# A residual-add LayerNorm on one core: the wait for the last store moves from SyncE's queue to TensorE's

## The chip, the cores and the metric

The kernel runs on one core of one Trainium2 chip. The metric is device time in microseconds (us), the median over several executions. With it comes, for every execution, the *span*: the time from the first to the last instruction of the kernel that the trace records. The device time is a little longer than the span, that difference called the *remainder* below. Spans of timed runs are given to 0.1 us, so the remainder of one run is good to 0.05 us, and a mean over several runs to less.

## The reference

```python
batch, seq, dim = 16, 1024, 512          # x and residual, float32
z = x + residual
mean = np.mean(z, axis=-1, keepdims=True)
var = np.var(z, axis=-1, keepdims=True)
return gamma * (z - mean) / np.sqrt(var + eps) + beta
```

The inputs are 2 x 33.55 MB and the output is 33.55 MB.

## The kernel before

SyncE issues all large transfers, GpSimd adds the residual, ScalarE takes the sums for mean and variance, VectorE normalises in place. TensorE does almost nothing: at the start it spreads gamma and beta over 128 partitions with two small matmuls. The kernel ends with SyncE waiting until the stores have landed and clearing all the semaphores that it used, so that the next execution finds zeros.

```python
OUT_CHUNKS = [16] * 7 + [8, 4, 4]            # rows per partition of each store
...
so = [sem(f"so{c}") for c in range(len(stores))]   # one semaphore per store, the last allocated
nums = [s.num for s in sems]
...
# TensorE: all that it does
nc.tensor.wait_ge(s_const, 1)
for k, dest in enumerate((gamma_p, beta_p)):
    nc.tensor.wait_ge(s_gb[k], 16)
    nc.tensor.matmul(dest[:, :], ones[:, :], gb_row[:, k * D : (k + 1) * D], start=True, stop=True
    ).then_inc(s_pe, 1)
...
# SyncE, after its last store was issued
for o, (lo, n) in enumerate(stores[:-1]):
    if lo >= stored:
        nc.sync.wait_ge(so[o], 16)
nc.sync.sem_clear(range(nums[0], nums[-1]))             # all but the last semaphore
nc.sync.wait_ge(so[-1], 16)                             # the last store
nc.sync.sem_clear(range(nums[-1], nums[-1] + 1))        # its semaphore
```

A store's semaphore reaches 16 by sixteen increments. In the trace those of the last store come one by one, from 236.15 to 238.33 us.

## Time and profile before

| | before |
|---|---|
| device time, median of the first 3 runs | 239.53 us (239.42 to 239.70) |
| the profiled run: time, span, remainder | 239.69, 238.37, 1.32 us |
| DMA queue q1, share of 16 engines | 99.1% |
| busiest compute engine (ScalarE) | 186.5 us, 78% |
| busy TensorE | 3.7 us |

The first lines are from the profile's page of the kernel before. The first gives the span, the second each engine's busy time and share; the DMA row shows the busy share of the DMA engines in 40 equal slices, in tenths; the last line is the queue's share.

```profile
span 238.4 us, 1803 instructions
PE 3.7 (2%) x4; PEld 1.2 (0%) x4; DVE 177.2 (74%) x290; ACT 186.5 (78%) x545; POOL 142.2 (60%) x21
...
DMA  8999999999999999999999999999999999999996
...
q1 hardware_dynamic: 6336, 100.67, 99.1%
```

The DMA engines are full in every slice but the first and the last, so the transfers bound the kernel, and the change doesn't touch them. The next view is the list of SyncE's own waits in the window from 228 us to the end: the waiting line, what it waited for, us in total, number of waits, the longest.

```profile
SPq L138 <- DVE zbuf L243: 5.9, 1, 5.9
SPq L166 <- DMA out_dram<-zbuf: 4.6, 2, 2.4
SPq L169 <- DMA out_dram<-zbuf: 2.3, 1, 2.3
```

L138 issues the last store once VectorE (DVE) is done; L166 are the waits for the stores before it, L169 the wait for the last. The instructions themselves, from the views of the two clearing lines: duration in ns (smallest, median, largest), and when the first and last of them started.

```profile
L167 SPq EVENT_SEMAPHORE_RANGE_CLEAR  x1: 118/118/118, 235.9 to 235.9; - x1
...
L169 SPq EVENT_SEMAPHORE_RANGE_CLEAR  x1: 25/25/25, 238.3 to 238.3; - x1
```

The wait itself is not part of the duration. The Trainium skill says so of such instructions ("Perfetto Trace Analysis", "Sequencer-only Instruction (DRAIN, etc)": the reported window is the execution alone, after the semaphores are satisfied), and this trace agrees: SyncE waited 2.3 us there and 25 ns are reported. The clear of L169 is the last instruction of the span.

One more view of the kernel before, the barrier at its opening (L55), lets one compare the engines at the same kind of instruction.

```profile
L55 SPq EVENT_SEMAPHORE  x2: 17/17/17, 1.5 to 1.8; - x2
...
L55 PEldq EVENT_SEMAPHORE  x2: 51/51/51, 1.5 to 1.8; - x2
```

PEldq is TensorE's sequencer. Its semaphore instruction takes three times as long as SyncE's.

### The profile page before, as it was taken

How to read it: one execution, taken by the hardware profiler on the slowest of the kernel's cores; microseconds unless marked ns; L12 is line 12 of the kernel's file. 1: busy time of each engine (PE TensorE's matmuls, PEld its weight loads, DVE VectorE, ACT ScalarE, POOL GpSimd, SP SyncE). 2: the span in 40 equal slices, each digit the busy share in tenths (PEclk: the TensorE clock that was granted, in tenths of full speed). 3: DMA queues.
4: the chain of work that ended last, by engine and by line, in shares of the span. 5: the costliest groups of instructions: out<-in, count | busy, mean ns of one | idle time of the engine just before them, and what ended most of it. 6: DMA issues, size and time to landing. Idle time of an engine off the chain costs nothing.

```text
span 238.4 us, 1803 instructions
## 1 busy us (share of the span) xinstructions
PE 3.7 (2%) x4; PEld 1.2 (0%) x4; DVE 177.2 (74%) x290; ACT 186.5 (78%) x545; POOL 142.2 (60%) x21
## 2 busy tenths in 40 slices
PE   0600000000000000000000000000000000000000
PEld 0100000000000000000000000000000000000000
DVE  0000488888888889998888888887888648888870
ACT  2003999999999999999999999989997399999700
POOL 0098988989889407893088930889209892770000
DMA  8999999999999999999999999999999999999996
GB/s 308 438 429 415 437 437 429 426 423 437 429 429 418 440 434 426 459 434 396 429 429 429 434 429 429 426 470 434 390 434 418 434 440 408 472 434 434 390 425 257
DMA packets 6340, 100.67 MB, mean 422 GB/s; under 512 B 706, under 2 KB 706, under 8 KB 708
## 3 DMA queue, kind: packets, MB, share of 16 engines
q1 hardware_dynamic: 6336, 100.67, 99.1%
q10 hardware_dynamic: 4, 0.00, 0.0%
HBM read 67.11 MB, written 33.55 MB: 422 GB/s over the span
## 4 chain that ended last, share of the span: by engine, by line
ACT 38%; DMA 33%; issue 10%; POOL 7%; ACTq 5%; DVE 3%; SPq 1%; DVEq 0%; POOLq 0%
DMA rbuf<-in_residual_dram 21%; ACT junk_s L203 20%; ACT junk_m L194 18%; DMA out_dram<-zbuf 12%; POOL zbuf L181 7%; ACTq L194 2%; DVE zbuf L228 2%; DVE zbuf L243 1%; ACTq L203 1%; SPq L138 1%; ACTq L189 1%; ACT std L211 0%; ACTq L201 0%; ACTq L210 0%; DVEq L228 0%
## 5 line engine op out<-in xcount | busy, mean ns | idle before, releaser
L181 POOL TENSOR_TENSOR zbuf<-zbuf,rbuf 128x4096 f32<-128x4096 f32 (+1 forms) x17 | 142.0, 8353 | 70.9 <-DMA rbuf<-in_residual_dram 70.9
L228 DVE SCALAR_TENSOR_TENSOR zbuf<-zbuf,nm,gamma_p 128x512 f32 x128 | 87.1, 743 | 50.4 <-ACT junk_s L203 50.4
L194 ACT ACTIVATE junk_m<-zbuf 128x512 f32 x128 | 74.9, 585 | 28.5 <-POOL zbuf L181 23.3
L203 ACT ACTIVATE junk_s<-zbuf,nm 128x512 f32 x128 | 88.8, 694 | 3.9
L243 DVE SCALAR_TENSOR_TENSOR zbuf<-zbuf,rstd,beta_p 128x512 f32 x128 | 87.1, 744 | 1.1
L203 ACT ACTIVATION_READ_ACCUMULATOR junk_s<-zbuf,nm x128 | 23.9, 187 | 0.0
L194 ACT ACTIVATION_READ_ACCUMULATOR junk_m<-zbuf x128 | 23.9, 187 | 0.0
L211 ACT ACTIVATE std<-ssq,eps_t x32 | 9.5, 297 | 3.7
L237 DVE RECIPROCAL rstd<-std x32 | 5.4, 170 | 0.0
L187 ACT ACT_TABLE_LOAD x1 | 1.3, 1283 | 2.7 <-PEq L55 2.7
L123 PE MATMUL gamma_p<-gb_row,ones 1*128 1x512 f32 x2 | 2.0, 1122 | 7.3 <-DMA gb_row<-in_gamma_dram 7.3
L123 PE MATMUL beta_p<-gb_row,ones 1*128 1x512 f32 x2 | 1.9, 1056 | 0.0
L118 DVE MEMSET ones<- 1x128 f32 x1 | 0.2, 165 | 2.0 <-PEq L55 2.0
L123 PEld LDWEIGHTS beta_p<-gb_row,ones 1*128 1x128 f32 x2 | 0.7, 332 | 1.0 <-DMA gb_row<-in_beta_dram 0.5
L123 PEld LDWEIGHTS gamma_p<-gb_row,ones 1*128 1x128 f32 x2 | 0.5, 305 | 7.3 <-issue 7.3
L278 POOL MEMSET const-float32-0.0<- 128x1 f32 x1 | 0.1, 99 | 0.2 <-issue 0.2
L278 POOL MEMSET const-bfloat16-1.0<- 128x1 bf16 x1 | 0.1, 101 | 0.0
L278 POOL MEMSET const-uint8-127<- 128x1 uint8 x1 | 0.1, 101 | 0.0
L278 POOL MEMSET const-float32-1.0<- 128x1 f32 x1 | 0.1, 98 | 0.0
L119 DVE MEMSET eps_t<- 128x1 f32 x1 | 0.1, 59 | 0.0
## 6 DMA issues: line engine op xcount, KB each, us to landing
zbuf<-in_x_dram SPq DMA_DIRECT2D x15, 2048.0 KB, 32.8
rbuf<-in_residual_dram SPq DMA_DIRECT2D x15, 2048.0 KB, 30.1
out_dram<-zbuf SPq DMA_DIRECT2D x7, 4096.0 KB, 28.6
zbuf<-in_x_dram SPq DMA_DIRECT2D x2, 1024.0 KB, 32.6
rbuf<-in_residual_dram SPq DMA_DIRECT2D x2, 1024.0 KB, 34.6
out_dram<-zbuf SPq DMA_DIRECT2D x1, 2048.0 KB, 15.0
out_dram<-zbuf SPq DMA_DIRECT2D x2, 1024.0 KB, 9.4
gb_row<-in_gamma_dram ACTq DMA_DIRECT2D x1, 2.0 KB
```

Source lines behind the costliest of these rows:

```text
L123: nc.tensor.matmul(dest[:, :], ones[:, :], gb_row[:, k * D : (k + 1) * D], start=True, stop=True).then_inc(s_pe, 1)
L138: i = nc.sync.dma_start(out=out, in_=in_).then_inc(s, 16)
L181: nc.gpsimd.tensor_tensor(out=z, in0=z, in1=part(rbuf, R_ROWS, a, an), op=ALU.add).then_inc(s_add, an)
L187: act.preload_act_table_set("sqrt_and_others")
L189: with act.Fori(0, turns) as t:
L194: act.activation(out=junk_m[k][:, :], in_=zbuf[:, bass.ds(zoff + k * D, D)], func=ACT.Identity, scale=-inv_d, accum_out=nm[:, bass.ds(r0 + ...
L203: act.activation(out=junk_s[k][:, :], in_=zbuf[:, bass.ds(zoff + k * D, D)], func=ACT.Square, bias=nm[:, bass.ds(r0 + k, 1)], accum_out=ss ...
L211: act.activation(out=std[:, bass.ds(r0, TURN)], in_=ssq[:, bass.ds(r0, TURN)], func=ACT.Sqrt, bias=eps_t[:, 0:1], scale=inv_d,).then_inc(s ...
L228: dve.scalar_tensor_tensor(out=row, in0=row, scalar=nm[:, bass.ds(r0 + k, 1)], in1=gamma_p[:, :], op0=ALU.add, op1=ALU.mult,)
L237: dve.reciprocal(out=rstd[:, bass.ds(r0, TURN)], in_=std[:, bass.ds(r0, TURN)]).then_inc(s_dve, TURN)
L243: dve.scalar_tensor_tensor(out=row, in0=row, scalar=rstd[:, bass.ds(r0 + k, 1)], in1=beta_p[:, :], op0=ALU.mult, op1=ALU.add,).then_inc(s_ ...
L278: nc = _bacc.Bacc("TRN2", target_bir_lowering=False, num_devices=1)
```

## The change

The last store's wait and the clear of its semaphore are issued on TensorE, which has had nothing to do since about 11 us. Nothing says that TensorE is better for it; the question is what the place of these two instructions is worth.

```diff
     nc.sync.sem_clear(range(nums[0], nums[-1]))
-    nc.sync.wait_ge(so[-1], 16)
-    nc.sync.sem_clear(range(nums[-1], nums[-1] + 1))
+    nc.tensor.wait_ge(so[-1], 16)
+    nc.tensor.sem_clear(range(nums[-1], nums[-1] + 1))
```

## The prediction

> **What bounds the kernel now.** The DMA engines. The page's row of DMA slices reads 9 tenths in 38 of 40 slices, queue q1 is busy 99.1% of 16 engines' span; no compute engine is over 78% (ACT 186.5 us, DVE 177.2, POOL 142.2, PE 3.7 of 238.4 us). The change touches no transfer, no arithmetic and no wait that frees a buffer.
>
> **The end as it stands** (instructions and semaphore events of the trace). The last normalise ends on DVE at 230.8 us, and the last 1 MB store is issued on SyncE at 230.81. SyncE then waits for the earlier stores (events at 233.38 and 235.82), clears all semaphores but the last at 235.91 (118 ns), and waits 2.3 us for the last store (list of SyncE's waits, L169). Fifteen of its sixteen increments are there by 236.81, the sixteenth at 238.33: one DMA engine lags with single 8 KB packets of 0.31 us until 237.87. The one-semaphore clear starts at 238.348, 15 ns after that increment, takes 25 ns, and is the span's last instruction.
>
> **What changes.** That clear leaves SyncE's stream and becomes TensorE's last instruction. TensorE, idle after the second gamma/beta matmul (about 11 us), parks on the last store's semaphore for some 227 us and delays nobody. SyncE is done 2.3 us earlier, after the big clear at about 236.0. The last store's landing is not moved.
>
> So only the reaction to the last increment and the clear itself change engine, some 40 ns in all, fully on the critical path. The opening barrier shows both at the same thing: released together (SyncE starts at 1.182 us, TensorE at 1.194), its semaphore instruction takes 17 ns on SyncE and 51 ns on TensorE. I estimate from this that reaction plus clear goes from 40 ns to 80 to 130 ns: +0.04 to +0.1 us in the span.
>
> **Outside the span.** The measured 239.53 us is 1.1 us longer than the span. The Trainium skill ("Runtime: NRT & Kernel Launch", "The ~15µs preamble/postamble breakdown") says that a barrier after the kernel waits for all engines. If so, only the last engine counts, and SyncE's being early gains nothing; this trace stops at the last clear and cannot show it. The ending may be longer or shorter on TensorE; with 1.1 us at stake, I give that at most half a microsecond either way.
>
> **Prediction.** 239.6 us, 8 in 10 within 239.2 to 240.0. Faster by over 2%: 0.01; within 2%: 0.98; slower by over 2%: 0.01. Two per cent is 4.8 us, twice the wait that moves.
>
> **What would show it right or wrong.** Right: the compute groups the same within 0.5 us; the last store issued at about 230.8 us and landed at about 238.3; SyncE's last instruction the big clear near 236.0; TensorE's clear within 0.15 us of the sixteenth increment and last in the span. The step "only reaction and clear change" is wrong if the last increment itself moves by over 0.3 us, or TensorE's clear starts late or takes over 0.2 us. The step on the time outside the span is wrong if measured time minus span leaves 1.1 us by over 0.3.
>
> **What would make it wrong.** A TensorE that wakes slowly after 227 us; an ending outside the trace that is dearer or cheaper on TensorE; the big clear on SyncE now ending its stream and letting something of the ending overlap the last 2.3 us (a gain of up to 1 us). None reaches 2%.

## The result and the profile after

| | before | after |
|---|---|---|
| device time, median of 4 runs | 239.49 us (239.42 to 239.70) | 239.97 us (239.77 to 240.39) |
| ratio after/before, 95% interval | | 1.0021 (1.0004 to 1.0038) |
| the profiled run: time, span, remainder | 239.69, 238.37, 1.32 us | 239.98, 238.39, 1.59 us |
| remainder, mean over the runs with both (least to most) | 1.32 (one run) | 1.58 (1.57 to 1.59, 4 runs) |

A ratio is the mean time of one kernel's fast runs over that of the other's fast runs of the same rounds, so it is not quite the ratio of the medians in the table. All runs were at a granted clock of 1.0. The experiments ran in three sets of rounds, on chips 7, 13 and 9; the remainder of the kernel before was 1.31, 1.31 and 1.30 us there, so remainders are compared across the sets.

The interval leaves 1 out: the changed kernel is slower by a fifth of a per cent. The page of the changed kernel, in the lines that answer to those above:

```profile
span 238.4 us, 1803 instructions
PE 3.7 (2%) x4; PEld 1.2 (0%) x4; DVE 177.2 (74%) x290; ACT 186.5 (78%) x545; POOL 142.2 (60%) x21
...
DMA  8999999999999999999999999999999999999996
...
q1 hardware_dynamic: 6336, 100.67, 99.1%
```

These are the same, digit for digit. SyncE's waits in the last 10 us have lost one row:

```profile
SPq L138 <- DVE zbuf L243: 5.9, 1, 5.9
SPq L166 <- DMA out_dram<-zbuf: 4.7, 2, 2.4
```

And from the views of the two clearing lines of the changed kernel:

```profile
L167 SPq EVENT_SEMAPHORE_RANGE_CLEAR  x1: 118/118/118, 235.9 to 235.9; - x1
...
L169 PEldq EVENT_SEMAPHORE_RANGE_CLEAR  x1: 63/63/63, 238.3 to 238.3; - x1
```

The clear stands on TensorE now and takes 63 ns in place of 25. And the instructions of the trace hold no more than that: the events of the two traces (instruction starts, and the increments of the last store's semaphore, in us) line up to 0.05 us, but for the fifteenth increment, which came 0.11 us earlier.

```
                                         before     after
last store issued by SyncE              230.811   230.770
fifteenth increment of its semaphore    236.806   236.696
sixteenth increment                     238.331   238.296
the clear starts                        238.348   238.324
the clear ends = end of the span        238.373   238.387
```

From the sixteenth increment to the end of the span it is 42 ns before and 91 ns after, 0.05 us more. The medians differ by 0.48 us. The rest is not in the instructions of the trace; between the two profiled runs 0.27 us of it is in the remainder. (The traces do hold semaphore events after the end of the span; they are read after the five points of the section on the prediction.)

### The profile page after: what moved, and what is told of

It is laid out like the page before. It is cut to its first block, busy times and chain, and to the rows that moved or that the text cites. A ratio compares the mean times of both kernels' runs of the same rounds, so it can differ in the third digit from the quotient of the medians.

```text
span 238.4 us, 1803 instructions
## 1 busy us (share of the span) xinstructions
PE 3.7 (2%) x4; PEld 1.2 (0%) x4; DVE 177.2 (74%) x290; ACT 186.5 (78%) x545; POOL 142.2 (60%) x21
## 4 chain that ended last, share of the span: by engine, by line
ACT 38%; DMA 33%; issue 10%; POOL 7%; ACTq 5%; DVE 3%; SPq 1%; DVEq 0%; POOLq 0%
DMA rbuf<-in_residual_dram 21%; ACT junk_s L203 20%; ACT junk_m L194 18%; DMA out_dram<-zbuf 12%; POOL zbuf L181 7%; ACTq L194 2%; DVE zbuf L228 2%; DVE zbuf L243 1%; ACTq L203 1%; SPq L138 1%; ACTq L189 1%; ACT std L211 0%; ACTq L201 0%; ACTq L210 0%; DVEq L228 0%
```

## The experiments

The theories:

- **A**: after its last instruction each engine has an ending that the trace doesn't show. TensorE's is longer than SyncE's.
- **B**: what costs is that SyncE is not the last any more, whoever takes its place.
- **C**: TensorE is slow because it was parked for 227 us.
- **N**: the difference is scatter of the DMA part.

Later A was divided: **P**, the endings run side by side and the last to finish counts; **S**, only the engine that comes last counts; **W**, the engine that the last store's semaphore releases counts; **Q**, a fixed addition whenever another engine than SyncE is released by the last store.

### The changed kernel again

No edit. It ran in the same rounds as the next three kernels and 11 runs of the kernel before.

> The changed kernel once more, unedited. Measured time minus span was 1.32 us for the profiled run of the kernel before and 1.58 us for that of the changed one. Theory A (after the last clear there is an ending that the trace doesn't show, and it is dearer when TensorE is the engine that comes last): time minus span 1.5 to 1.7 us in every run, time 0.2 to 0.5 us over the kernel before. Theory N (the 0.48 us between the medians was scatter of the DMA part): time minus span 1.3 us in some runs, time within 0.15 us of the kernel before.

Measured: 240.22 us median against 239.82 us, ratio 1.0014 (1.0001 to 1.0027). The mean span is 238.62 us against 238.58 us, so hardly different. The remainder is 1.60 us (1.57 to 1.63 in 5 runs) against 1.31 us (1.27 to 1.37 in 11 runs). The two ranges don't touch, although the times overlap. N falls as the cause of the remainder. The scatter of the time is in the span: the kernel before ranges over 0.9 us there, and a quantity that leaves the span out is much sharper.

### The last wait and clear on each other engine

The edit, here for ScalarE, placed after that engine's loop; VectorE (`nc.vector`) and GpSimd (`nc.gpsimd`) likewise.

```diff
     nc.sync.sem_clear(range(nums[0], nums[-1]))
-    nc.sync.wait_ge(so[-1], 16)
-    nc.sync.sem_clear(range(nums[-1], nums[-1] + 1))
 ...
+    nc.scalar.wait_ge(so[-1], 16)
+    nc.scalar.sem_clear(range(nums[-1], nums[-1] + 1))
```

> The last wait and clear on ScalarE, after its loop (it ends at about 225 us). Theory A1 (the ending depends on which engine comes last): a value of time minus span of its own, between 1.2 and 1.7 us, the same in every run. Theory B (what costs is that SyncE is no longer last and its early end helps nothing or harms): 1.58 us like TensorE. Theory C (TensorE is slow because it was parked for 227 us, cold): ScalarE worked until 225 us, so 1.3 us as SyncE. The clear itself starts within 0.1 us of the sixteenth increment under all.

> The last wait and clear on VectorE, after its loop (it ends at 230.8 us). Theory A1: a value of time minus span of its own, between 1.2 and 1.7 us. Theory B: 1.58 us. Theory C: 1.3 us. The clear takes 25 to 60 ns.

> The last wait and clear on GpSimd, after its last addition (it ends at about 213 us). Theory A1: a value of time minus span of its own, between 1.2 and 1.7 us. Theory B: 1.58 us. Theory C: 1.3 us, or a little over, since it is parked for 25 us.

The clears, one line from each kernel's view of its clearing line (ACTq is ScalarE, DVEq VectorE, POOLq GpSimd). ScalarE:

```profile
L252 ACTq EVENT_SEMAPHORE_RANGE_CLEAR  x1: 41/41/41, 238.3 to 238.3; - x1
```

VectorE:

```profile
L252 DVEq EVENT_SEMAPHORE_RANGE_CLEAR  x1: 55/55/55, 238.4 to 238.4; - x1
```

GpSimd:

```profile
L252 POOLq EVENT_SEMAPHORE_RANGE_CLEAR  x1: 48/48/48, 238.5 to 238.5; - x1
```

| last engine | sixteenth increment to end of span | remainder, mean (least to most) | runs | median time | ratio (95%) |
|---|---|---|---|---|---|
| SyncE (before) | 0.04 us | 1.31 (1.27 to 1.37) | 11 | 239.82 | |
| VectorE | 0.08 | 1.43 (1.40 to 1.48) | 5 | 239.92 | 1.0002 (0.9989 to 1.0015) |
| ScalarE | 0.06 | 1.48 (1.47 to 1.51) | 6 | 240.17 | 1.0023 (1.0004 to 1.0043) |
| TensorE | 0.09 | 1.60 (1.57 to 1.63) | 5 | 240.22 | 1.0014 (1.0001 to 1.0027) |
| GpSimd | 0.07 | 1.86 (1.81 to 1.90) | 6 | 240.36 | 1.0021 (1.0009 to 1.0034) |

The second column is from the profiled run of each kernel (the one of before is the first of the study). Each engine has a remainder of its own, steady to 0.06 us about its mean. That is what A expects, although GpSimd's 1.86 us lies outside the 1.2 to 1.7 us that were forecast for it. B wants one value for the four that are not SyncE, and they range from 1.43 to 1.86 us. C wants SyncE's value for the engines that worked almost to the end; VectorE, busy until 230.8 us, has 1.43 us and GpSimd has the largest of all. The medians and ratios do not order the engines: ScalarE's ratio is the largest because three of its six runs happened to have spans of 238.9 to 239.7 us. Nor is the order that of the visible clear: GpSimd's clear is shorter than VectorE's and TensorE's, and its remainder is the longest.

### TensorE woken before the end

VectorE signals a new semaphore after its loop, and TensorE does one more matmul on that signal, before it waits for the last store. In this and in all the kernels below the new semaphore `s_late` is allocated after the stores' semaphores, and the last clear covers both.

```diff
-    nc.sync.sem_clear(range(nums[0], nums[-1]))
-    nc.sync.wait_ge(so[-1], 16)
-    nc.sync.sem_clear(range(nums[-1], nums[-1] + 1))
+    nc.sync.sem_clear(range(nums[0], nums[-2]))
+    nc.tensor.wait_ge(s_late, 1)
+    nc.tensor.matmul(gamma_p[:, :], ones[:, :], gb_row[:, 0:D], start=True, stop=True)
+    nc.tensor.wait_ge(so[-1], 16)
+    nc.tensor.sem_clear(range(nums[-2], nums[-1] + 1))
 ...
+    late_t = nc.alloc_sbuf_tensor("late_t", [P, 1], FP32)      # after VectorE's loop
+    nc.vector.memset(late_t[:, :], 0.0).then_inc(s_late, 1)
```

> The changed kernel, but TensorE is woken at 231 us by VectorE's end and does one more matmul (128x512, into a tile that nobody reads any more) before it waits for the last store: it then is parked for 5 us, not for 227. Theory C (long parking makes TensorE's ending slow): time minus span 1.31 to 1.40 us. Theories P and S: 1.60 us, as before.

The view of the added matmul's line shows that TensorE did work at 231 us (it is recorded as two passes):

```profile
L170 PE MATMUL gamma_p<-gb_row,ones x2: 1056/1136/1215, 230.9 to 231.9; 1*128 1x512 f32 x2
```

Measured: remainder 1.59 us (1.57 to 1.62, 4 runs) against 1.31 us (1.28 to 1.35, 7 runs); median 240.09 against 239.79 us, ratio 1.0027 (1.0000 to 1.0054). C falls: parked for 5 us or for 227 us, TensorE's remainder is the same.

### Half of the change: TensorE waits, SyncE clears

```diff
-    nc.sync.sem_clear(range(nums[0], nums[-1]))
-    nc.sync.wait_ge(so[-1], 16)
-    nc.sync.sem_clear(range(nums[-1], nums[-1] + 1))
+    nc.sync.sem_clear(range(nums[0], nums[-2]))
+    nc.tensor.wait_ge(so[-1], 16)
+    nc.tensor.sem_inc(s_late, 1)
+    nc.sync.wait_ge(s_late, 1)
+    nc.sync.sem_clear(range(nums[-2], nums[-1] + 1))
```

> Half of the change alone: TensorE waits for the last store and then signals SyncE, which clears. SyncE is last by one hop, which I expect to take 0.05 to 0.15 us. Time minus span was 1.31 us on average with SyncE last and 1.60 us with TensorE last. Theory P (each engine has its own ending, they run side by side, and the measured time stops when the last of them is done; TensorE's is some 0.3 us longer): TensorE's ending still is the last one, so time minus span is 1.60 us less the hop, 1.45 to 1.57 us. Theory S (only which engine comes last counts): 1.31 us. Theory W (whoever is released by the last store's semaphore counts): 1.60 us.

From the views of its two last lines:

```profile
L170 PEldq EVENT_SEMAPHORE  x1: 51/51/51, 239.0 to 239.0; - x1
...
L172 SPq EVENT_SEMAPHORE_RANGE_CLEAR  x1: 31/31/31, 239.1 to 239.1; - x1
```

Measured: SyncE's clear ends 0.06 us after TensorE's signal does, and is the last in the trace. The remainder is 1.56 us (1.55 to 1.56, 4 runs) against 1.31 us for the kernel before; median 240.21 against 239.79 us, ratio 1.0018 (1.0001 to 1.0034). S expected 1.31 and falls: SyncE is last and the remainder is not SyncE's. P expected 1.60 less the hop, which with the measured 0.06 us is 1.54. W expected 1.60, only 0.04 us away; this run alone doesn't separate P from W.

### The other half: SyncE waits, TensorE clears

```diff
-    nc.sync.sem_clear(range(nums[0], nums[-1]))
+    nc.sync.sem_clear(range(nums[0], nums[-2]))
     nc.sync.wait_ge(so[-1], 16)
-    nc.sync.sem_clear(range(nums[-1], nums[-1] + 1))
+    nc.sync.sem_inc(s_late, 1)
+    nc.tensor.wait_ge(s_late, 1)
+    nc.tensor.sem_clear(range(nums[-2], nums[-1] + 1))
```

> The other half alone: SyncE waits for the last store, signals TensorE, and TensorE clears and is last. Theories P and S: time minus span 1.60 us, as in the changed kernel, and the span longer by the hop of 0.05 to 0.15 us, so 0.4 us over the kernel before in all. Theory W (the engine that the last store releases counts): 1.31 us.

From the views of its two last lines:

```profile
L170 SPq EVENT_SEMAPHORE  x1: 17/17/17, 238.9 to 238.9; - x1
...
L172 PEldq EVENT_SEMAPHORE_RANGE_CLEAR  x1: 63/63/63, 238.9 to 238.9; - x1
```

Measured: remainder 1.57 us (1.56 to 1.58, 4 runs), median 240.22 us, ratio 1.0017 (1.0000 to 1.0033). The end of the span is 0.13 us after the sixteenth increment. W expected 1.31 us here and falls: TensorE is not released by the store, and its ending is still there. Each half of the change alone brings the whole cost, since each leaves TensorE among the engines that end at the very end.

### GpSimd waits, SyncE clears

As the first half, with the wait and the signal on GpSimd after its last addition (added lines only):

```diff
+    nc.sync.sem_clear(range(nums[0], nums[-2]))
+    nc.sync.wait_ge(s_late, 1)
+    nc.sync.sem_clear(range(nums[-2], nums[-1] + 1))
 ...
+    nc.gpsimd.wait_ge(so[-1], 16)
+    nc.gpsimd.sem_inc(s_late, 1)
```

> As the first, with GpSimd in TensorE's place, whose ending was the longest (1.86 us). Theory P: 1.86 us less the hop of 0.05 to 0.15 us, so 1.70 to 1.81 us, although SyncE is last in the trace. Theory S: 1.31 us. The two are four times as far apart as the hop, so this is the sharper test.

From the views of its two last lines:

```profile
L255 POOLq EVENT_SEMAPHORE  x1: 17/17/17, 238.6 to 238.6; - x1
...
L170 SPq EVENT_SEMAPHORE_RANGE_CLEAR  x1: 31/31/31, 238.7 to 238.7; - x1
```

Measured: remainder 1.83 us (1.80 to 1.88, 4 runs), with SyncE's clear ending 0.06 us after GpSimd's signal; median 240.48 against 239.79 us, ratio 1.0033 (1.0017 to 1.0050). S (1.31 us) is half a microsecond off. P's rule with this hop gives 1.80 us; the mean lies 0.02 us above the range that was forecast for P.

### GpSimd first, SyncE later by a known time

What was still open was whether the endings overlap (P) or whether GpSimd's part is a fixed addition (Q). SyncE is held back after GpSimd by signalling itself, five times or fourteen (added lines only; the loop takes the place of the single wait for `s_late`).

```diff
+    for k in range(5):                       # 14 in the second kernel
+        nc.sync.wait_ge(s_late, k + 1)
+        nc.sync.sem_inc(s_late, 1)
+    nc.sync.wait_ge(s_late, 5 + 1)
     nc.sync.sem_clear(range(nums[-2], nums[-1] + 1))
```

> GpSimd waits for the last store and signals SyncE, as in the last kernel with GpSimd; SyncE then signals itself five times, one after the other, before it clears, so that it ends later than GpSimd by D. I expect D of about 0.3 us, and the trace shows it. Theory P (endings side by side; the last to finish counts): time minus span is the larger of 1.31 us and 1.87 us less D, so about 1.55 us. Theory Q (having GpSimd released by the last store adds a fixed 0.5 us, whatever SyncE does after it): 1.83 us still.

> The same with fourteen such signals, D of about 0.8 us. Theory P: GpSimd's ending is over before SyncE's, so time minus span is back at SyncE's own 1.31 us. Theory Q: 1.83 us.

From the views of three lines of the kernel with five signals, GpSimd's signal, SyncE's five and the clear:

```profile
L258 POOLq EVENT_SEMAPHORE  x1: 17/17/17, 238.8 to 238.8; - x1
...
L171 SPq EVENT_SEMAPHORE  x5: 17/17/17, 238.8 to 239.1; - x5
...
L173 SPq EVENT_SEMAPHORE_RANGE_CLEAR  x1: 31/31/31, 239.2 to 239.2; - x1
```

And of the kernel with fourteen:

```profile
L258 POOLq EVENT_SEMAPHORE  x1: 17/17/17, 238.6 to 238.6; - x1
...
L171 SPq EVENT_SEMAPHORE  x14: 17/17/17, 238.7 to 239.5; - x14
...
L173 SPq EVENT_SEMAPHORE_RANGE_CLEAR  x1: 31/31/31, 239.6 to 239.6; - x1
```

The delays D between the end of GpSimd's signal and the end of SyncE's clear came out longer than expected, 0.42 and 1.02 us. P's rule with these is the larger of 1.31 and 1.87 - D, that is 1.45 and 1.31 us. Measured: 1.49 us (1.46 to 1.51, 4 runs) and 1.36 us (1.31 to 1.38, 4 runs), beside 1.30 us (1.28 to 1.33, 7 runs) for the kernel before. Q's 1.83 us falls. The medians are 240.80 and 241.14 against 240.20 us, the ratios 1.0025 (1.0009 to 1.0042) and 1.0048 (1.0029 to 1.0067): the delay itself shows there, as it must. The second mean is 0.05 us above SyncE's own; that little is unexplained. In the profiled run, with the span taken to the nanosecond, it is 1.33 against 1.32 us for the first kernel of the study.

Counted from the sixteenth increment the runs fit together. Each row adds the visible part, from the profiled run, to the mean remainder.

| kernel | visible | remainder | sum |
|---|---|---|---|
| SyncE alone (before) | 0.04 | 1.31 | 1.35 us |
| TensorE alone (the changed kernel, again) | 0.09 | 1.60 | 1.69 |
| TensorE waits, SyncE clears 0.06 us later | 0.14 | 1.56 | 1.70 |
| GpSimd alone | 0.07 | 1.86 | 1.93 |
| GpSimd waits, SyncE clears 0.06 us later | 0.10 | 1.83 | 1.93 |
| the same, SyncE 0.42 us later | 0.46 | 1.49 | 1.95 |
| the same, SyncE 1.02 us later | 1.06 | 1.36 | 2.42 |

As long as SyncE is late by less than the difference of the two endings (0.55 us for GpSimd), its delay is swallowed, and the sum stays at 1.93 to 1.95 us. Beyond that SyncE decides, and the sum goes up to near 1.06 + 1.31 = 2.37 us.

## Why the prediction was right, and the term that was mis-sized

The measured 239.97 us lies in the predicted range of 239.2 to 240.0 us, near its upper end, and the call "within 2%" held. That it fell inside the range is in part luck: it is 0.03 us from the edge, and in the next rounds the same kernel had a median of 240.22 us, outside it (the kernel before had 239.82 us there, 0.29 us over the value from which the prediction started). The forecast rise was about 0.07 us, the measured one is some 0.34 us. Point by point:

1. *The kernel is bound by the DMA engines and the change touches no transfer.* Right. The page's lines are the same, and the sixteenth increment came at 238.331 us before and 238.296 us after.
2. *Parking TensorE for 227 us delays nobody.* Right; waking it at 231 us changed neither its reaction (28 ns in both) nor the remainder.
3. *Reaction and clear go from 40 ns to 80 to 130 ns.* Right: 42 ns became 91 ns. The estimate from the opening barrier, 17 ns against 51 ns for the same instruction, was a good guide: the clear went from 25 to 63 ns.
4. *SyncE's being early gains nothing.* Right, and now shown, not only argued from the Trainium skill: an early SyncE hides its own ending, but the measured time stops with the last ending of all. The skill ("Runtime: NRT & Kernel Launch", "The ~15µs preamble/postamble breakdown") has a barrier after the kernel that waits for all engines. The runs agree with a wait for the last one, in that 0.42 us of SyncE's delay vanished behind GpSimd, and the traces hold a chain of semaphore updates that waits for all five engines (below). That this chain is the page's barrier is likely; the trace doesn't name it.
5. *The ending outside the span.* This is the step that was mis-sized. The prediction saw that it could be "longer or shorter on TensorE", put nothing into the sum for it, and gave it half a microsecond either way. It is 0.29 us longer on TensorE than on SyncE (1.60 against 1.31 us, same rounds), about six times the visible 0.05 us that the prediction did count. The prediction's base was off too: it took 1.1 us, the median time less the span of another run, where the remainder of the profiled run is 1.32 us. By the text's own test (a change of over 0.3 us from 1.1) this step is wrong, though 0.22 us of that 0.49 us is the base; from 1.32 us it is 0.27 us.

The sum from the measured terms is 0.05 us visible and 0.29 us in the remainder, 0.34 us in all; 239.53 + 0.34 = 239.87 us would have been the prediction. In the second set of rounds the mean times differ by 0.32 us (240.22 less 239.90) and the mean spans by 0.04, which fits. The first comparison's medians differ by 0.48 us. I put the excess of 0.14 us down to scatter of the span, since the changed kernel's four spans there ranged from 238.2 to 238.8 us; with one span for the kernel before in those rounds, that is likely and not shown.

**What the traces hold after the span.** The prediction says that the trace stops at the last clear, and the experiments treated the ending as unseen. But the packed traces also keep semaphore events, which no view of `prof` lists. Semaphore 2, which no instruction of the program names, is updated nine times as the engines finish and nine times more at the very end. The trace doesn't say which engine makes an update; the times tell. In the kernel before, the first five come at 11.24 us (0.17 us after TensorE's last matmul), at 225.53 (0.11 us after ScalarE's last instruction), at 225.57 (for GpSimd, done since 213.38), at 230.93 (0.15 us after VectorE's last) and at 238.50 (0.12 us after SyncE's clear). Four more follow within 0.16 us, from 238.54 to 238.66. I read this as a chain from TensorE to SyncE and back, in which each step waits for the one before. An engine that is done early has its step behind it, and an engine that is last holds up all steps after its own.

| last engine | its first step, after its last instruction | steps after that | ninth step, after the end of the span | remainder of the profiled run |
|---|---|---|---|---|
| SyncE (before) | 0.125 us | 4 | 0.289 us | 1.32 us |
| VectorE | 0.146 | 5 | 0.395 | 1.43 |
| ScalarE | 0.113 | 7 | 0.447 | 1.48 |
| TensorE (the changed kernel, again) | 0.195 | 8 | 0.562 | 1.59 |
| GpSimd | 0.527 | 6 | 0.820 | 1.85 |

From the ninth step to the eighteenth it is 1.15 us in each of the twelve traces, and the remainder less the fourth column is 1.02 to 1.04 us in each, so the whole difference between the engines arises before the ninth step. TensorE's 0.27 us over SyncE is 0.07 us for a later first step and 0.20 us for eight further steps in place of four: it stands at the head of the chain, SyncE at its turning point. GpSimd stands in the middle, and costs most because its first step comes so late (0.56 us after a signal, in the three kernels in which it signals SyncE). In the kernel with fourteen signals, GpSimd's and VectorE's steps were done 0.41 us before the span ended, and the ninth came 0.287 us after it, as with SyncE alone. So both things were at work: a delay of each engine's own, which runs beside the others', and a common chain in which the engines stand at different places. An estimate of 0.19 us could have been read beforehand from the trace of the kernel before: its second chain takes 0.36 us from the first step to the ninth, and its first chain 0.16 us from SyncE's step to the ninth.

What stays open is why GpSimd takes so long to its first step, and what the engines do between the two chains.

No version beats the kernel before. SyncE has the shortest remainder of the five engines and the shortest clear, so of the places tried the last wait was in its best one already.

## What to carry to other kernels

What the last instruction's engine does after it is part of the measured time and not part of the span, so in a kernel like this one give the last wait to the engine with the shortest ending (here SyncE, 0.12 to 0.55 us ahead of the others), and don't let another engine end within that distance of the end. For a question of a few tenths of a microsecond, compare measured time minus span run by run: that stood within 0.06 us of its mean while the time itself scattered by up to 1.4 us. When a change seems to move only a wait, ask which engine then ends last, and look for the cost outside the span as well as in it. The semaphore events after the span, in traces already taken, held here what ten experiments were made to corner.

## What the Trainium skill lacked or had wrong

- "Runtime: NRT & Kernel Launch", "The ~15µs preamble/postamble breakdown", gives what follows the kernel as one figure for all engines (about 1.5 us for the barrier, 1.5 us for the semaphore reset, 2 us for the last part). It lacks that the cost depends on the engine that ends last: in these runs, time minus span is 1.31 us for SyncE, 1.43 for VectorE, 1.48 for ScalarE, 1.60 for TensorE and 1.86 for GpSimd. It also lacks where each engine stands in that barrier, and each engine's own delay before it (0.11 to 0.53 us here). The page's three parts add up to 5 us; in these traces the last semaphore event comes 1.44 us (SyncE) to 1.97 us (GpSimd) after the last instruction, after two chains of nine steps and, between them, updates of nearly all the semaphores from 7 to 255. Whether these are the page's parts is not shown.
- "Perfetto Trace Analysis", "Sequencer-only Instruction (DRAIN, etc)", gives no durations by engine. Here the same one- or two-semaphore clear takes 25 to 31 ns on SyncE, 41 on ScalarE, 48 on GpSimd, 55 on VectorE and 63 on TensorE.
- "DMA: Bandwidth & Descriptors", "Anatomy of one DMA — SWDGE (gpsimd) path", says, of that path, that most of a transfer's fixed 2 us is the wait for the write's receipt. The stores here take another path, and the 2.3 us that the kernel waits at its end looks like it and mostly is not: fifteen of the last store's sixteen increments are there at 236.81 us and the sixteenth at 238.33, and from 236.44 us on only one packet of 8 KB is under way at a time, 0.31 us each, until 237.86, which looks like one DMA engine that had fallen behind. Its lag, taken as the time from the fifteenth increment to the sixteenth, was 0.07 us at the load that landed at 7.45 us, 0.31 us at 115.25 us, 0.97 us at 206.24 us and 1.52 us at the end. The same page, "Latency and other measured facts", does say that DMA engines 7 and 15 are usually slower than the others; it gives no figure for how far one falls behind, and the packed traces don't say which engine it was here. The lag was there in all twelve traces (1.39 to 1.93 us at the end), and no experiment looked for its cause.
